# Expert selection beside the query products, and the gathered tile's second-table rows summed by TensorE

## The chip, the cores and the metric

One core of a Trainium2 chip runs the whole kernel. Its engines have queues of their own: TensorE (PE in the profile; its weight loads are PEld), VectorE (DVE), ScalarE (ACT), GpSimd (POOL) and SyncE (SP), which issues most transfers. The metric is the device time of one execution in microseconds, lower is better, compared by the median of several runs.

## The reference, cut to what matters

One layer over 512 tokens of width 2048: a token mixer (state space and pooling), and then an expert network, to which the change belongs. Each token has 8 heads; a head takes the best 16 of 128 first keys and of 128 second keys, sums them to 256 candidates and keeps the best 16, so a token has 128 picks among 128 x 128 single-neuron experts.

```python
q = (hb @ w_q).reshape(PEER_BLOCK, PEER_HEADS, 2, PEER_HALF)
s1 = jnp.einsum('thd,kd->thk', q[:, :, 0], k1).astype(jnp.float32)
s2 = jnp.einsum('thd,kd->thk', q[:, :, 1], k2).astype(jnp.float32)
v1, i1 = lax.top_k(s1, PEER_TOPK)
v2, i2 = lax.top_k(s2, PEER_TOPK)
...
top_s, pos = lax.top_k(cand, PEER_TOPK)
eid = jnp.take_along_axis(cid, pos, axis=-1)
g = jax.nn.softmax(top_s, axis=-1)
u_sel = jnp.take(u_tab, eid, axis=0)
act = jax.nn.gelu(jnp.einsum('td,thkd->thk', hb, u_sel).astype(jnp.float32)) * g
v_sel = jnp.take(v_tab, eid, axis=0)
return jnp.einsum('thk,thkd->td', act.astype(hb.dtype), v_sel)
```

The layer's output is x + g2 times this, followed by a final RMSNorm with weight final_w.

## The kernel before

The 512 tokens are four tiles of 128. All large products are done in three passes on operands split into a high and a low part (mm3, lines 109 to 112): `wload` (lines 117 to 132) loads a block of 128 x 1024 weights on SyncE's queue (wraw), ScalarE makes the high part (whi, line 125), and VectorE or GpSimd subtracts it to make the low part (wlo, line 126). Each wload is also a tick: side work is written as generators in lanes, and each tick advances a lane by its rate (line 199).

After the mixer come four stages. In `tail`, the output projection (accumulators pso), the second norm, and then the *query products* (psq, head by head) with their scores against the keys (pss). VectorE copies the scores out (sv) and GpSimd's queue sends them to a scratch in memory (scd).

`peer` is the expert network. Tiles 1 to 3 run dense: `dense_u` is the *expert scores* stage, products of the three tiles with the whole first table (psU, 384 columns, 128 second keys of two blocks each), and `dense_v` is the *weighted sum* stage, products with the whole second table (psV, 512 columns, 256 blocks). Tile 0 runs by gathered rows: `gather_tile` fetches for each pick one row of the first table for each of its 128 tokens (an indirect transfer of 1 MB issued by GpSimd), VectorE multiplies and sums it with the tokens (line 1095), ScalarE makes the weight, and then the row of the second table is fetched and VectorE adds it, weighted, to the tile's output (line 1088). This lane (lane0) runs through both stages at 0.29 and 0.25 picks a tick.

A second lane (lane1, 1.6 steps a tick) runs beside the expert scores: `topk` reads a tile's scores back and selects on VectorE (top16: five instructions for 8 + 8 values), tile 0 first; `dense_keys` and `dense_gates` then spread the dense tiles' gates with one-hot products (psd) into scratch. In both stages lo_pool gives the share of low parts that GpSimd makes, 0.5.

A scheduler orders each engine's instructions ahead of time by its own simulated timeline; on GpSimd, from `peer` on, the order is that of the code. At run time each engine works through its order. The gathered rows have three buffers (rows2), and psT are two PSUM banks for small results.

## Time and profile before

| | before |
|---|---|
| median of 3 runs | 3981.82 us |
| the runs | 3994.41, 3969.19, 3981.82 us |
| span of the profiled execution | 3959.9 us |
| busy: TensorE, VectorE, GpSimd, ScalarE | 3750.4, 2587.5, 1726.1, 1185.9 us |

The span runs from the first to the last instruction of the profiled execution. The execution's own device time is not listed on the page beside it; the runs without a profile lie 9.3 to 34.5 us above the span, the median 21.9 us. Times in the views are microseconds from the start of the span. The query products lie at 1391 to 1594 us, the expert scores from there to 2857, the weighted sum to 3942.

### The profile page before, as it was taken

Reading aid. Unit: us, or ns where it says so; the run is one execution under the profiler, and the core shown is the slowest. Engines: PE = TensorE matmul, PEld = TensorE weight load, DVE = VectorE, ACT = ScalarE, POOL = GpSimd, SP = SyncE. Lnnn points to the kernel's source line nnn. Section 1 sums busy time; section 2 is a strip of 40 time slices with the busy share of each in tenths; the row PEclk is TensorE's granted clock in tenths of the full one; section 3 lists DMA queues with packets and bytes.
Section 4 is the critical chain, followed back from the end, with each engine's and each line's share of the span. In section 5 each row is a group of like instructions: output and inputs, shape, how many; then the busy total and the mean of one; then the engine's idle time right before and its main releaser. Section 6 shows DMA issues by size and latency. Waiting matters only on the chain.

```text
span 3959.9 us, 49350 instructions
## 1 busy us (share of the span) xinstructions
PE 3750.4 (95%) x18841; PEld 3200.4 (81%) x18841; DVE 2587.5 (65%) x3347; ACT 1185.9 (30%) x1742; POOL 1726.1 (44%) x985
## 2 busy tenths in 40 slices
PE   5999998889899899999999999999999999999997
PEld 2478876667777778999999999999978788888886
DVE  5264379997563332899997777854666666566666
ACT  4123331112222222332333333323333333333332
POOL 0043125552322300355554344445566666666663
PEclk9999999989999999999999999999999999999999
DMA  8635658779865423477776777788888887888784
GB/s 270 212 120 185 206 169 232 222 221 302 241 223 186 141 86 112 149 255 272 281 263 254 272 262 275 256 297 297 302 306 293 311 296 284 306 312 292 281 310 173
DMA packets 458238, 962.81 MB, mean 243 GB/s; under 512 B 105040, under 2 KB 248784, under 8 KB 422416
## 3 DMA queue, kind: packets, MB, share of 16 engines
q1 hardware_dynamic: 380896, 588.77, 45.8%
q0 software_dynamic: 47744, 305.23, 20.7%
q10 hardware_dynamic: 29360, 65.64, 4.5%
q8 instruction: 148, 2.42, 0.3%
q14 instruction: 90, 0.74, 0.1%
HBM read 864.08 MB, written 99.12 MB: 243 GB/s over the span
## 4 chain that ended last, share of the span: by engine, by line
PE 54%; DVE 10%; DMA 3%; POOL 1%; issue 1%; SPq 0%; ACT 0%; DVEq 0%; POOLq 0%; ACTq 0%
PE psV L111 8%; PE psV L112 8%; PE psV L110 8%; PE psU L112 5%; PE psU L111 5%; PE psU L110 5%; PE psd L1151 3%; DVE wlo L126 2%; PE pso L111 2%; PE pso L110 2%; PE pso L112 2%; PE psq L111 1%; PE psq L112 1%; PE psq L110 1%; DMA row<-in_u,eid 1%; DVE row L1095 1%
## 5 line engine op out<-in xcount | busy, mean ns | idle before, releaser
L125 ACT CAST whi<-wraw 128x1024 fp32r<-128x1024 f32 x712 | 746.5, 1050 | 1779.0 <-PE psU L111 472.8
L126 DVE TENSOR_TENSOR wlo<-wraw,whi 128x1024 fp32r<-128x1024 f32 x456 | 643.8, 1412 | 648.4 <-ACT whi L125 307.6
L126 POOL TENSOR_TENSOR wlo<-wraw,whi 128x1024 fp32r<-128x1024 f32 x256 | 705.8, 2758 | 799.9 <-ACT whi L125 758.1
L112 PE MATMUL psU<-h2Th,wlo 128*128 128x384 f32 x2048 | 698.3, 341 | 28.6 <-DVE wlo L126 18.9
L110 PE MATMUL psU<-h2Th,whi 128*128 128x384 f32 x2048 | 698.8, 341 | 6.6 <-ACT whi L125 6.6
L111 PE MATMUL psU<-h2Tl,whi 128*128 128x384 f32 x2048 | 696.9, 340 | 0.0
L111 PE MATMUL psV<-wlo,ah 128*128 128x512 f32 x1536 | 606.5, 395 | 10.5 <-DVE wlo L126 5.9
L112 PE MATMUL psV<-whi,al 128*128 128x512 f32 x1536 | 605.4, 394 | 0.0
L110 PE MATMUL psV<-whi,ah 128*128 128x512 f32 x1536 | 554.4, 394 | 0.0
L112 PEld LDWEIGHTS psU<-h2Th,wlo 128*128 128x128 f32 x2048 | 389.7, 190 | 35.1 <-DVE wlo L126 23.2
L1095 DVE SCALAR_TENSOR_TENSOR row<-row,h 128x2048 f32<-128x2048 f32 x128 | 352.9, 2757 | 92.9 <-DMA row<-in_u,eid 92.9
L110 PEld LDWEIGHTS psU<-h2Th,whi 128*128 128x128 f32 x2048 | 391.1, 191 | 7.1 <-ACT whi L125 6.9
L111 PEld LDWEIGHTS psU<-h2Tl,whi 128*128 128x128 f32 x2048 | 390.2, 191 | 0.1
L111 PEld LDWEIGHTS psV<-wlo,ah 128*128 128x128 f32 x1536 | 289.8, 189 | 82.1 <-POOL wlo L126 8.3
L1088 DVE SCALAR_TENSOR_TENSOR ffn<-row,w,ffn 128x2048 f32<-128x2048 f32 x127 | 340.6, 2682 | 10.2 <-DMA row<-in_v,eid 10.2
L112 PEld LDWEIGHTS psV<-whi,al 128*128 128x128 f32 x1536 | 289.4, 188 | 67.0
L110 PEld LDWEIGHTS psV<-whi,ah 128*128 128x128 f32 x1536 | 289.1, 188 | 66.3
L1080 POOL DMA_INDIRECT row<-in_u,eid x128 | 209.0, 1633 | 247.7 <-ACT w L1096 97.5
L1080 POOL DMA_INDIRECT row<-in_v,eid x128 | 255.5, 1996 | 19.2 <-issue 7.0
L820 DVE SCALAR_TENSOR_TENSOR lacc<-lw,sil,lacc 128x512 f32<-128x512 f32 x240 | 213.6, 890 | 55.1 <-DMA lw<-in_w_mod 53.1
L112 PE MATMUL psg<-hhi,wlo 128*128 128x512 f32 x512 | 203.6, 402 | 25.5 <-DVE wlo L126 25.5
L110 PE MATMUL psg<-hhi,whi 128*128 128x512 f32 x512 | 203.8, 398 | 0.0
(350 smaller groups left out, 5537.2 us busy)
## 6 DMA issues: line engine op xcount, KB each, us to landing
wraw<-in_uT SPq DMA_DIRECT2D x256, 512.0 KB
wraw<-in_v SPq DMA_DIRECT2D x256, 512.0 KB
lw<-in_w_mod SPq DMA_DIRECT2D x256, 256.0 KB
wraw<-in_w_in SPq DMA_DIRECT2D x96, 512.0 KB
wmod<-in_w_mod SPq DMA_DIRECT2D x48, 512.0 KB
sd<-sev ACTq DMA_DIRECT2D x64, 384.0 KB
gds<-ast ACTq DMA_DIRECT2D x12, 2048.0 KB
sr<-sd SPq DMA_DIRECT2D x32, 768.0 KB
```

The source lines that it names most:

```text
L110: mm(ps, a.hi, b.hi, start=start, stop=False)
L111: mm(ps, a.hi, b.lo, start=False, stop=False)
L112: mm(ps, a.lo, b.hi, start=False, stop=stop)
L125: nc.scalar.copy(hi, raw)
L126: ins = (eng or nc.vector).tensor_tensor(lo, raw, hi.bitcast(F32), op=OP.subtract)
L820: nc.vector.scalar_tensor_tensor(acc, w, self.sil[:, k, 0:1], acc, op0=OP.mult, op1=OP.add)
L1080: nc.gpsimd.indirect_dma_start(out=r, out_offset=None, in_=I[tab], in_offset=bass.IndirectOffsetOnAxis(ap=eid[:, k:k + 1], axis=0))
L1088: V.scalar_tensor_tensor(acc, v, w, acc, op0=OP.mult, op1=OP.add)
L1095: V.scalar_tensor_tensor(u, u, 1.0, h2, op0=OP.mult, op1=OP.mult, accum_out=w[:, 0:1])
L1151: nc.tensor.matmul(ps[:, n * P:(n + 1) * P], oh[:, 0, :, n], R[:, q, :, n], start=(q == 0), stop=(q == 2))
```

## The change

The selection moves from `topk` into the loop over heads of the query products: ScalarE copies the scores, VectorE takes the best 16 of each of the four tiles' keys straight from the copy and then the best 16 of the candidates, head by head. The scratch scd, its writes and its reads are gone. The low parts of heads 1 to 7's query weights are made by GpSimd. What is left of `topk` (the keys of the picks and the softmax) is `picks`.

The gathered tile is worked in two halves. `gather_u`, beside the expert scores (lane0, 0.58 steps a tick), fetches all 128 rows of the first table and keeps the dot products; at the end it makes all weights at once and transposes weights and expert numbers, so that the picks lie on the partitions. `gather_v`, beside the weighted sum (0.56 steps a tick), fetches for each of the 128 *tokens* the 128 rows of the second table that it picked. A row block is then summed by TensorE: float32 products with a 128 x 32 weight tile (st) that is zero but for the column of this token, 512 columns each, one for each quarter of the 2048 output columns, at column positions 0, 32, 64 and 96 (psG). Groups of 32 tokens share an accumulator; at the end of each group the residual, the norm and the store follow in the same layout of quarters. In the weighted sum the share of GpSimd in the low parts falls from 0.5 to 0.34, and lane1 takes 1.1 steps a tick.

The core of the diff (comments that fell away are left out):

```diff
                 for kb in range(KT // 4):
-                    w = self.wchunk(I["peer_wq"], kb * 4, 4, hd * 256, 256)
+                    w = self.wchunk(I["peer_wq"], kb * 4, 4, hd * 256, 256, nc.gpsimd if hd else None)
                     for kk in range(4):
                         k = kb * 4 + kk
                         for j in range(2):
                             self.mm3(ps[j], w[:, kk, j * P:(j + 1) * P], h2T[:, k, :], k == 0, k == KT - 1)
                 for j in range(2):
-                    qt = ep.tile([P, SEQ], F32, tag="xr", name=self.nm("qt"), bufs=4)
+                    qt = ep.tile([P, SEQ], F32, tag="xr", name=self.nm("qt"))
                     nc.scalar.copy(qt, ps[j])
                     pss = self.psT.tile([P, 512], F32, tag="tr", name=self.nm("pss"))
                     for t in range(TT):
                         nc.tensor.matmul(pss[:, t * P:(t + 1) * P], qt[:, t * P:(t + 1) * P], self.kT[:, j, :], start=True, stop=True)
                     sv = ep.tile([P, SEQ], F32, tag="sv", name=self.nm("sv"))
-                    nc.vector.tensor_copy(sv, pss)
-                    nc.gpsimd.dma_start(self.scd[:, :, (hd * 2 + j) * P:(hd * 2 + j + 1) * P].rearrange("t p k -> p t k"),
-                                        sv.rearrange("p (t k) -> p t k", t=TT))
+                    nc.scalar.copy(sv, pss)
+                    for t in range(TT):
+                        junk = ep.tile([P, 256], F32, tag="tkj", name=self.nm("tkj"))
+                        self.top16(self.vv[t][:, hd, j], self.ii[t][:, hd, j], sv[:, t * P:(t + 1) * P], junk[:, 0:P])
+                for t in range(TT):
+                    cand = ep.tile([P, TOPK, TOPK], F32, tag="cand", name=self.nm("cand"))
+                    shp = [P, TOPK, TOPK]
+                    nc.vector.tensor_tensor(cand, self.vv[t][:, hd, 0].unsqueeze(2).broadcast_to(shp),
+                                            self.vv[t][:, hd, 1].unsqueeze(1).broadcast_to(shp), op=OP.add)
+                    junk = ep.tile([P, 256], F32, tag="tkj", name=self.nm("tkj"))
+                    self.top16(self.ts[t][:, hd], self.pos[t][:, hd], cand.rearrange("p a b -> p (a b)"), junk)
...
-        S = tp.tile([P, 2 * HEADS, P], F32, tag="S", name=self.nm("S"))
-        nc.sync.dma_start(S, self.scd[t].rearrange("p (h k) -> p h k", k=P))
...
-    def gather_tile(self, t, res, acc):
-        nc, I, V, h2 = self.nc, self.I, self.nc.vector, self.h2[t]
+    def gather_u(self, t, res, out):
+
+
+        nc, I, V, kp, h2 = self.nc, self.I, self.nc.vector, self.keep, self.h2[t]
         i1, i2, g = res[t]
-        ef = self.keep.tile([P, NK], F32, name=self.nm("ef"))
+        ef = kp.tile([P, NK], F32, name=self.nm("ef"))
         V.scalar_tensor_tensor(ef, i1, float(P), i2, op0=OP.mult, op1=OP.add)
-        eid = self.keep.tile([P, NK], I32, name=self.nm("eid"))
+        eid = kp.tile([P, NK], I32, name=self.nm("eid"))
         V.tensor_copy(eid, ef)
-
-        def row(tab, k):
-            r = self.rowp.tile([P, D], F32, tag="row", name=self.nm("row"))
-            nc.gpsimd.indirect_dma_start(out=r, out_offset=None, in_=I[tab],
-                                         in_offset=bass.IndirectOffsetOnAxis(ap=eid[:, k:k + 1], axis=0))
-            return r
-
-        def vacc(k, v, w):
-            if k == 0:
-                V.tensor_scalar(acc, v, w, None, op0=OP.mult)
-            else:
-                V.scalar_tensor_tensor(acc, v, w, acc, op0=OP.mult, op1=OP.add)
-
-        u, pend = row("u", 0), None
+        dots = kp.tile([P, NK], F32, name=self.nm("dots"))
+        u = self.row("u", eid, 0)
         yield
         for k in range(NK):
+            nxt = self.row("u", eid, k + 1) if k + 1 < NK else None
             with self.tc.issue_after(self.last_lo):
-                w = self.sm.tile([P, 4], F32, tag="w", name=self.nm("w"))
-                V.scalar_tensor_tensor(u, u, 1.0, h2, op0=OP.mult, op1=OP.mult, accum_out=w[:, 0:1])
-                nc.scalar.activation(w[:, 1:2], w[:, 0:1], AF.Gelu_apprx_tanh)
-                nc.scalar.activation(w[:, 2:3], w[:, 1:2], AF.Copy, scale=g[:, k:k + 1])
-                if pend is not None:
-                    vacc(*pend)
-            v = row("v", k)
-            pend = (k, v, w[:, 2:3])
-            if k + 1 < NK:
-                u = row("u", k + 1)
+                V.scalar_tensor_tensor(u, u, 1.0, h2, op0=OP.mult, op1=OP.mult, accum_out=dots[:, k:k + 1])
+            u = nxt
             yield
-        vacc(*pend)
...
+        nc.scalar.activation(dots, dots, AF.Gelu_apprx_tanh)
+        V.tensor_tensor(dots, dots, g, op=OP.mult)
+        ps = self.psT.tile([P, 512], F32, tag="tr", name=self.nm("pst"))
+        for j, x in enumerate((dots, ef)):
+            nc.tensor.transpose(ps[:, j * P:(j + 1) * P], x, self.ident)
+        wT = kp.tile([P, P], F32, name=self.nm("wT"))
+        nc.scalar.copy(wT, ps[:, 0:P])
+        eT = kp.tile([P, P], I32, name=self.nm("eT"))
+        V.tensor_copy(eT, ps[:, P:2 * P])
+        out.append((wT, eT))
+        yield
+
+    def row(self, tab, ids, k):
+        r = self.rowp.tile([P, D], F32, tag="row", name=self.nm("row"))
+        self.nc.gpsimd.indirect_dma_start(out=r, out_offset=None, in_=self.I[tab],
+                                          in_offset=bass.IndirectOffsetOnAxis(ap=ids[:, k:k + 1], axis=0))
+        return r
+
...
+        wT, eT = wt[0]
+        st = [kp.tile([P, 32, 32], F32, name=self.nm("st")) for _ in range(2)]
+        for x in st:
+            nc.vector.memset(x, 0.0)
...
+        rows = [self.row("v", eT, k) for k in range(2)]
+        yield
+        for g in range(4):
+            s = st[g % 2]
+            V.tensor_copy(s.rearrange("p a b -> p (a b)")[:, 0:32 * 32:33], wT[:, g * 32:(g + 1) * 32])
+            ps = self.psT.tile([P, 512], F32, tag="tr", name=self.nm("psG"))
+            for j in range(32):
+                k = g * 32 + j
+                if k + 2 < P:
+                    rows.append(self.row("v", eT, k + 2))
+                r = rows.pop(0)
+                for q in range(4):
+                    nc.tensor.matmul(ps[32 * q:32 * q + 32, :], s[:, j, :], r[:, q * 512:(q + 1) * 512],
+                                     start=(j == 0), stop=(j == 31), tile_position=(0, 32 * q))
+                yield
+            r0 = t * P + g * 32
+            x1 = kp.tile([P, 512], F32, tag="x1q", name=self.nm("x1q"))
+            for q in range(4):
+                nc.sync.dma_start(x1[32 * q:32 * q + 32], self.x1d[r0:r0 + 32, q * 512:(q + 1) * 512])
+            o = kp.tile([P, 512], F32, tag="outq", name=self.nm("outq"))
+            V.tensor_tensor(o, ps, g2, op=OP.mult)
+            V.tensor_tensor(o, o, x1, op=OP.add)
+            ss = self.sm.tile([P, 4], F32, tag="ssq", name=self.nm("ssq"))
+            nc.scalar.activation(x1, o, AF.Square, accum_out=ss[:, 0:1])
+            ps = self.psT.tile([P, 512], F32, tag="tr", name=self.nm("psn"))
+            nc.tensor.matmul(ps[:, 0:1], same.rearrange("p q j -> p (q j)"), ss[:, 0:1], start=True, stop=True)
+            nc.scalar.activation(ss[:, 1:2], ps[:, 0:1], AF.Sqrt, bias=self.epsb, scale=1.0 / D)
+            V.reciprocal(ss[:, 2:3], ss[:, 1:2])
+            V.scalar_tensor_tensor(o, o, ss[:, 2:3], fw, op0=OP.mult, op1=OP.mult)
+            for q in range(4):
+                nc.sync.dma_start(self.out[r0:r0 + 32, q * 512:(q + 1) * 512], o[32 * q:32 * q + 32])
             yield
-            self.add_half(t, acc, dh, self.ss[0])
-        yield
-        self.finish(t, acc, self.ss[0])
 
...
-                yield from self.topk(tp, 0, res)
-                self.lane0[2].append(self.gather_tile(0, res, acc0))
+                yield from self.picks(self.tkp, 0, res)
+                self.lane0[2].append(self.gather_u(0, res, wt))
                 for t in DT:
-                    yield from self.topk(tp, t, res)
+                    yield from self.picks(self.tkp, t, res)
                     yield from self.dense_keys(t, res, ix)
...
-            self.lane0 = lane0 = self.lane(0.29, [])
-            lane1 = self.lane(1.6, [prep()])
+            self.lane0 = lane0 = self.lane(0.58, [])
+            lane1 = self.lane(1.1, [prep()])
...
-            lane0[0], self.lo_pool = 0.25, 0.5
+            lane0, self.lo_pool = self.lane(0.56, [self.gather_v(0, wt)]), 0.34
```

How the change stands in the engines' orders, at three places. First TensorE early in the weighted sum, at the change from one weight block to the next (psV are the accumulators, ah and al the split weights of the experts, whi and wlo the table's block). Before:

```order
L111 MATMUL psV_23277<-wlo_23451,ah_23278 128x512
L112 MATMUL psV_23277<-whi_23450,al_23279 128x512
L110 MATMUL psV_23272<-whi_23474,ah_23278 128x512
L110 MATMUL psV_23273<-whi_23474,ah_23278 128x512
L110 MATMUL psV_23274<-whi_23474,ah_23278 128x512
```

And now, at the same products:

```order
L111 MATMUL psV_23099<-wlo_23301,ah_23100 128x512
L112 MATMUL psV_23099<-whi_23300,al_23101 128x512
L1138 MATMUL psG_23211<-row_23212,st_23139 32x512 x4
L110 MATMUL psV_23094<-whi_23324,ah_23100 128x512
L110 MATMUL psV_23095<-whi_23324,ah_23100 128x512
L110 MATMUL psV_23096<-whi_23324,ah_23100 128x512
```

The four quarter products of one token's rows stand between two blocks; the weighted sum's own products are as many as before.

Second, VectorE at the start of the expert scores. Before, the scores of the last head are copied out, the low part of the third second key's first block follows (wlo_12122), and tile 0's selection comes behind it:

```order
L126 TENSOR_TENSOR wlo_11956<-wraw_11954,whi_11955 128x1024
L126 TENSOR_TENSOR wlo_12041<-wraw_12039,whi_12040 128x1024
L1006 COPY sv_11895<-pss_11890 128x512
L1006 COPY sv_11905<-pss_11900 128x512
L126 TENSOR_TENSOR wlo_12122<-wraw_12120,whi_12121 128x1024
L1019 MAX vv_11962<-S_11960 128x8 x6
L1020 MAX_INDEX ii_11963<-vv_11962,S_11960 128x8
```

Now (ts and pos are the best candidates of a tile, oh and rf belong to picks, wlo_12669 is the low part of the fourth block that TensorE takes):

```order
L1033 MAX_INDEX pos_10799<-ts_10795,cand_12552 128x8
L1034 MATCH_REPLACE tkj_12554<-ts_10795,cand_12552 128x256
L1048 CAST rf_12604<-ri_12601 128x256
L1035 MAX ts_10794<-tkj_12546 128x8
L1035 MAX ts_10795<-tkj_12554 128x8
L1052 TENSOR_TENSOR oh_12607<-rf_12604,iota 128x2048
L1036 MAX_INDEX pos_10798<-ts_10794,tkj_12546 128x8
L1036 MAX_INDEX pos_10799<-ts_10795,tkj_12554 128x8
L1055 TENSOR_TENSOR oh_12607<-oh_12607,iif_12599 128x2048
L126 TENSOR_TENSOR wlo_12669<-wraw_12667,whi_12668 128x1024
```

The low part now stands behind the last head's selection of all four tiles and behind two steps of picks for tile 0.

Third, GpSimd in the weighted sum. Before (rows of both tables in turn, between low parts):

```order
L1080 DMA row_24599<-in_v,eid_12933 128x2048
L1080 DMA row_24601<-in_u,eid_12933 128x2048
L126 TENSOR_TENSOR wlo_24663<-wraw_24661,whi_24662 128x1024
L126 TENSOR_TENSOR wlo_24711<-wraw_24709,whi_24710 128x1024
L1080 DMA row_24720<-in_v,eid_12933 128x2048
L1080 DMA row_24722<-in_u,eid_12933 128x2048
```

And now (sr is the product of scores and gates of the dense tiles):

```order
L1245 TENSOR_TENSOR sr_23938<-sr_23938,gr_23939 128x12x4x32
L126 TENSOR_TENSOR wlo_24074<-wraw_24072,whi_24073 128x1024
L1102 DMA row_24078<-in_v,eT_22265 128x2048
L1102 DMA row_24108<-in_v,eT_22265 128x2048
L126 TENSOR_TENSOR wlo_24158<-wraw_24156,whi_24157 128x1024
```

Rows of the second table alone are fetched, by the transposed expert numbers (eT), and one low part stands between two pairs of rows where there were two.

## Rows read from the trace of the kernel before

**Rows 1.** The page, busy time, share of the span and instructions of each engine.

```profile
PE 3750.4 (95%) x18841; PEld 3200.4 (81%) x18841; DVE 2587.5 (65%) x3347; ACT 1185.9 (30%) x1742; POOL 1726.1 (44%) x985
```

**Rows 2.** The windows view, by stage (start:end, length, then by column).

```profile
core 0: us, PE busy (x) PEld busy (x) DVE busy (x) ACT busy (x) POOL busy (x), PEclk, DMA share, GB/s
1391.50:1594.00 202.50, 201.02 (x965) 167.22 (x964) 63.45 (x68) 47.92 (x60) 13.22 (x16) 1.00 0.32 100
1594.00:1970.00 376.00, 354.34 (x1963) 349.36 (x1962) 347.99 (x797) 118.43 (x167) 180.32 (x77) 0.97 0.69 243
1970.00:2620.00 650.00, 641.52 (x4026) 626.74 (x4025) 510.45 (x602) 221.12 (x350) 289.14 (x131) 0.99 0.73 264
2620.00:2857.00 237.00, 228.22 (x1298) 226.75 (x1297) 119.33 (x73) 74.72 (x112) 125.65 (x58) 0.99 0.84 301
2857.00:3942.00 1085.00, 1072.74 (x4611) 867.32 (x4609) 693.92 (x453) 342.60 (x420) 687.76 (x282) 1.00 0.80 290
3942.00:3960.00 18.00, 0.00 (x0) 0.00 (x0) 13.34 (x18) 4.22 (x9) 0.00 (x0) 0.52 0.52 204
```

**Rows 3.** The windows view of one tile each: psV, psU (PE, PEld, others), psd.

```profile
3100.00:3300.00 200.00, 199.95 (x863) 161.86 (x863) 11.44 (x18) 1.00 0.85 310
...
2700.00:2780.00 80.00, 78.49 (x452) 78.17 (x451) 4.34 (x9) 1.00 0.81 293
...
2420.00:2600.00 180.00, 42.82 (x324) 15.64 (x27) 1.00 0.75 268
```

**Rows 4.** The waits view of TensorE, 1594 to 2857: total us, times, longest.

```profile
PE psU L112 <- DVE wlo L126: 18.9, 9, 4.0
PE psU L112 <- POOL wlo L126: 9.6, 7, 3.0
```

**Rows 5.** The same, 2857 to 3960.

```profile
PE psV L111 <- DVE wlo L126: 5.9, 2, 4.9
PE psV L111 <- POOL wlo L126: 4.6, 6, 1.7
```

**Rows 6.** The groups by line, VectorE, 2857 to 3960: busy, mean ns, idle before.

```profile
L1095 DVE SCALAR_TENSOR_TENSOR row<-row,h 128x2048 f32<-128x2048 f32 x61 | 190.4, 3122 | 50.8 <-DMA row<-in_u,eid 50.7
...
L1088 DVE SCALAR_TENSOR_TENSOR ffn<-row,w,ffn 128x2048 f32<-128x2048 f32 x62 | 175.3, 2828 | 9.5 <-DMA row<-in_v,eid 9.5
```

**Rows 7.** The windows view of tile vv (first level), then of ts (second).

```profile
1594.00:2120.00 526.00, 103.88 (x516) 0.97 0.70 247
...
1594.00:2120.00 526.00, 68.69 (x260) 0.97 0.70 247
```

**Rows 8.** The groups by line, 1391 to 1594, VectorE's own.

```profile
L126 DVE TENSOR_TENSOR wlo<-wraw,whi 128x1024 fp32r<-128x1024 f32 x32 | 40.7, 1273 | 104.3 <-PE psq L112 99.2 <-ACT whi L125 5.1
...
L1006 DVE COPY sv<-pss 128x512 f32<-128x512 f32 x16 | 11.1, 691 | 30.1 <-PE pss L1004 30.1
```

**Rows 9.** The timeline of TensorE, first stage: start us, us, instruction.

```profile
107.97 0.39 PE L110 MATMUL psz<-whi,chi 128*128 128x512 f32 x1
108.28 1.05 PE L244 MATMUL psmod<-wmod,silz 128*32 128x512 f32 x4
...
109.61 0.40 PE L112 MATMUL psz<-whi,clow 128*128 128x512 f32 x1
```

**Rows 10.** The same, earlier (L343 is a float32 transpose).

```profile
42.21 0.62 PE L244 MATMUL psmod<-wmod,silz 128*32 128x256 f32 x4
42.77 1.09 PE L343 MATMUL pst<-ident,xt 128*128 128x128 f32 x8
...
45.37 1.06 PE L244 MATMUL psmod<-wmod,silz 128*32 128x256 f32 x12
```

**Rows 11.** The transfers, 2857 to 3942: issues, median us to landing.

```profile
row<-in_v,eid POOLq DMA_INDIRECT x61, 8.9
```

**Rows 12.** The timeline of TensorE in the query products (39 starts apart).

```profile
1455.09 0.39 PE L110 MATMUL psq<-h2Th,whi 128*128 128x512 f32 x1
...
1464.02 0.39 PE L110 MATMUL psq<-h2Th,whi 128*128 128x512 f32 x1
```

More of the change, by code (lines that the diff above doesn't have):

```diff
@@ L284, in mixers @@
         self.x1d = self.dram.tile([SEQ, D], F32, name="x1d")
-        self.scd = self.dram.tile([TT, P, 2 * HEADS * P], F32, name="scd")
         es_h, es_b = self.es(), self.es()
@@ L990, in tail @@
             self.h2T = h2T = Split(th, tl)
+            es_x.close()
+            ep = es.enter_context(pool(name="ev4", bufs=2))
+            self.es_e, self.es_t = self.es(), self.es()
+            self.evp = self.es_e.enter_context(pool(name="sev", bufs=2, side="right"))
+            self.tkp = tkp = self.es_t.enter_context(pool(name="topk", bufs=1, side="right"))
+            self.vv = [tkp.tile([P, HEADS, 2, TOPK], F32, name=f"vv{t}") for t in range(TT)]
+            self.ii = [tkp.tile([P, HEADS, 2, TOPK], U32, name=f"ii{t}") for t in range(TT)]
+            self.ts = [tkp.tile([P, HEADS, TOPK], F32, name=f"ts{t}") for t in range(TT)]
+            self.pos = [tkp.tile([P, HEADS, TOPK], U32, name=f"pos{t}") for t in range(TT)]
             for hd in range(HEADS):
@@ new lines, in tail, with top16, picks @@
+        self.check("q")
+    def top16(self, vals, idx, src, junk):
+        V = self.nc.vector
+        V.max(out=vals[:, 0:8], in_=src)
+        V.max_index(out=idx[:, 0:8], in_max=vals[:, 0:8], in_values=src)
+        V.match_replace(out=junk, in_to_replace=vals[:, 0:8], in_values=src, imm_value=-3.0e38)
+        V.max(out=vals[:, 8:16], in_=junk)
+        V.max_index(out=idx[:, 8:16], in_max=vals[:, 8:16], in_values=junk)
+    def picks(self, tp, t, res):
+        nc, V = self.nc, self.nc.vector
+        ts, pos, shp = self.ts[t], self.pos[t], [P, HEADS, TOPK, TOPK]
+        iif = tp.tile([P, HEADS, 2, TOPK], F32, tag="iif", name=self.nm("iif"))
+        V.tensor_copy(iif, self.ii[t])
@@ new lines, in quarters, with gather_v @@
+    def quarters(self, pool, ap, name):
+        t = pool.tile([P, 512], F32, name=name)
+        for q in range(4):
+            self.nc.sync.dma_start(t[32 * q:32 * q + 32], ap[:, q * 512:(q + 1) * 512].broadcast_to([32, 512]))
+        return t
+    def gather_v(self, t, wt):
+        nc, I, V, kp = self.nc, self.I, self.nc.vector, self.keep
+        wT, eT = wt[0]
+        st = [kp.tile([P, 32, 32], F32, name=self.nm("st")) for _ in range(2)]
+        for x in st:
+            nc.vector.memset(x, 0.0)
+        g2, fw = self.quarters(kp, self.modd[:, 3 * D:4 * D], "g2q"), self.quarters(kp, I["final_w"], "fwq")
+        same = kp.tile([P, 4, 32], F32, name="same")
+        V.tensor_reduce(same[:, 0], self.ident.rearrange("p (q j) -> p j q", q=4), axis=AX.X, op=OP.add)
+        for q in range(1, 4):
+            V.tensor_copy(same[:, q], same[:, 0])
+        rows = [self.row("v", eT, k) for k in range(2)]
[27 more added lines that the diff above has]
+            V.scalar_tensor_tensor(o, o, ss[:, 2:3], fw, op0=OP.mult, op1=OP.mult)
+            for q in range(4):
+                nc.sync.dma_start(self.out[r0:r0 + 32, q * 512:(q + 1) * 512], o[32 * q:32 * q + 32])
@@ L1325, in peer @@
             es_k.close()
-        self.hp.close()
 def build(tc, I, out, dbg=None, stop=None):
```

48 lines of the change are left out of this document (11 added, 37 removed).

## The prediction, made before the changed kernel ran

> **What bounds the kernel now.** I read the first part of the page first: TensorE is busy for 95% of the span and VectorE for 65% [rows 1]; the median of the runs, 3981.8 us, lies 21.9 us above that span. A share of busy time says little by itself, so I cut the span into stages with the windows view [rows 2]. The reader is to see that TensorE is busy for 201.0 of the 202.5 us of the query products, for 1224.1 of the 1263 us of the expert scores (three windows), and for 1072.7 of the 1085 us of the weighted sum; the granted clock is 0.97 to 1.00 there, which is the 2.4 GHz level. VectorE is over 90% busy only in the first window of the scores (348.0 of 376 us).
>
> Busy TensorE need not be TensorE at its pace, so I priced one product in the windows where nothing is late [rows 3]: 200.0/863 = 0.232 us for one of the weighted sum (512 columns), 78.5/452 = 0.174 us for one of the scores (384 columns), 42.8/324 = 0.132 us for a spread-gate product. The weighted sum has 3 x 1536 = 4608 products: 4608 x 0.232 = 1069 of its 1085 us. The scores' windows hold 7287 products; 1152 of them are the spread gates' (3 tiles, 128 tokens, 3 parts), so 6135 x 0.174 + 1152 x 0.132 = 1067 + 152 = 1219 of 1263 us. So, whatever is taken off the other engines, TensorE can get back about 44 us in the scores and 16 us in the weighted sum. The waits agree: 28.5 us of idle TensorE in the scores were ended by a low part of a weight block, and 10.5 us in the weighted sum [rows 4, 5]. TensorE is the bound from the queries on, and the tail of 18 us behind it stays as it is.
>
> **What is taken away.** VectorE loses the products with the second table's rows: 175.3 us in the weighted sum, and a like time in the scores; the dot products with the first table's rows (190.4 us in the weighted sum) all move into the scores, where they take the place of the row sums that leave [rows 6]. In the weighted sum VectorE, now 693.9 us busy, falls to 693.9 - 175.3 - 190.4 = 328 us, plus some 40 low parts that the new share (0.34 on GpSimd instead of 0.5) hands back to it. None of this was on the path: of the 12.3 us that TensorE idles there, 10.5 us are late low parts. I credit 6 us; the bounds are 0 and 12.
>
> **The selection.** It moves beside the query products. Today its two levels take 103.9 + 68.7 = 172.6 us of VectorE (the sums of candidates are among them) [rows 7]. The query stage gives VectorE 202.5 us and uses 63.5; the change takes away 28 of 32 low parts at 1.273 us and 16 copies of 11.1 us in all [rows 8], so VectorE would hold 63.5 - 35.6 - 11.1 + 172.6 = 189 us there. Per head that is 21.6 us of selection beside 25.3 us of products: it keeps up, and TensorE waits for none of it, since the low parts of heads 1 to 7 are on GpSimd and ScalarE copies the scores. I cost the stage at nothing; the cover is thin, and if it is gone, each microsecond that a head's selection takes over 25.3 us holds back the second of the two score buffers, then ScalarE's next high part, then TensorE.
>
> The end of the stage is where it shows. The last head's selection, 21.6 us, starts when its scores exist, that is when TensorE is already in the expert scores. In the order of VectorE's instructions the fourth block of the scores (its low part is wlo_12669 in the order above) stands behind nearly all of it and two steps of the picks. TensorE reaches that block after 72 products, 72 x 0.174 = 12.5 us; VectorE after about 21.6 + 5 + 1.3 = 28 us: a wait of some 16 us. The next blocks stand behind steps of the picks, for some 15 us more. Against this goes what the selection costs today in the same place: the first window of the scores has 376 us for 1963 products of 0.174 us = 341 us, 35 us lost. So nearly a wash: I credit 5 us, with bounds of 40 us gained (the selection out of the way, the boundary hidden) and 15 us lost.
>
> **The new products.** This is the term that decides. For each of the 128 tokens of the gathered tile TensorE now does four float32 products, 32 weight columns by 512 columns, one for each quarter of the output's columns, at four column positions. The trace of before has this form in the first stage: 32-column float32 products of the conditioning. Two of them, 512 columns, are four records (two passes each) over 1.05 us, and they stand between products that otherwise start every 0.23 us: from the product at 107.97 to that at 109.61 us are 1.64 us, where two starts would take 0.46, so the pair costs 1.18 us of TensorE's time [rows 9]. Do products at different positions run side by side? A full-width float32 transpose is two passes of 128 columns; four of them take 1.09 us, so a pass takes about 0.11 us, 0.22 for 256 columns. A pair at 256 columns, four passes, took 0.62 us, where one after the other would be 0.9: two run at once, a round of 0.43 and a fixed 0.19. Do four? Six such products at alternating positions (0 and 32, then 64 and 96) took 1.06 us, which is two rounds and 0.19, where pairs alone would need three (1.48) [rows 10]. So four at different positions run as one round, and a token costs 1.18 us. In TensorE's new order 118 tokens stand as one group of four; ten are broken by other products into 24 pieces, so 142 groups: 142 x 1.18 = 168 us. The bounds are the bare rounds of 512 columns, 128 x 0.86 = 110 us, and pairs that don't overlap with other pairs, 128 x 2 x 1.18 = 302 us; I take the row's price, being that of the same form. Nothing hides them: they are on the engine that sets the end, in a stage with 16 us to spare. The change breaks even only at (44 + 16)/128 = 0.47 us a token.
>
> The Trainium skill, page "TensorE: Matmul & The Clock Gate", section "Part 3: Packing small matmuls", speaks against the full packing: it gives a measured speedup of 2.38 for three column tiles of 32 with 512 columns, so a pack takes 3/2.38 = 1.26 times one product. By that, as an estimate, a group would take 1.05 x 1.26 + 0.13 = 1.45 us and the term 206 us instead of 168. The row with six products shows no such surcharge, and no run here shows four at 512 columns.
>
> Around them: four small products for the norms and two transposes, under 2 us. The gathers themselves do not grow: 128 rows a stage where there were about 130, and a row lands 8.9 us after its issue [rows 11]. TensorE now waits for rows itself, and 18 products of the weighted sum queue behind each late one. In the new order a row's products stand at least 54 products, 12.5 us, behind the group that frees its buffer, mostly 90 to 108 (over 20 us); so few are late. On GpSimd a row's issue waits for that group too, and behind it wait the low parts; they are needed 55 products (12.7 us) later or more, in which an issue and a low part fit. I cost this at nothing, with an upper bound in the rivals.
>
> **The sum.** 168 + 2 - 6 - 5 = +159 us: a span of about 4119 us, and with the 21.9 us that lie around it 4141 us, 4.0% slower. The low end takes the pieces as free (128 x 1.05 = 134), the full 40 us in the scores and 12 in the weighted sum: +82. For the high end I let a quarter of the 118 whole groups run as pairs, since the rows leave the four-wide round at 512 columns open: (142 + 30) x 1.18 = 203, + 2 + 15 = +220.
>
> **The rivals.** (a) *TensorE's pace rises.* At one column a cycle of the 2.4 GHz level 512 columns would be 0.213 us, and the weighted sum's product takes 0.232: 4608 x 0.019 = 86 us that could be operands arriving late while VectorE and GpSimd, both some 64% busy there, use the same memory. With VectorE at half its load they could come back; with these and both stages' bounds (12 and 40 us instead of 6 and 5) the sum is 159 - 86 - 41 = +32 us, 4014 us: not slower. It decides from the point where most of those 0.019 us go. Against it: the query products have 512 columns too, with VectorE 31% and GpSimd 7% busy, and their pace is 8.93/39 = 0.229 us [rows 12], so hardly 0.003 us a product, 14 us, hang on the neighbours' load. (b) *The four don't pack.* Pairs only: 302 - 9 = +293, 4275 us; no packing, with some 1 us for each, +450. For it: the row of six is one place, at 256 columns; against it: that row has no room for three rounds. (c) *TensorE waits for rows.* If every third token waited 3 us for its rows or for a low part behind an issue, 128 us come on top: 4270 us. For it: transfers already take 80% of the stage's DMA time; against it: the slack in the order. (d) *Selection bounds the queries.* If a head's selection took 30 us instead of 21.6, 8 x 4.7 = 38 us: 4180 us, inside the range.
>
> **How the numbers follow.** This kernel's runs spread over 0.6%, so a change within 1% can hardly be told from none; I count 3942 to 4022 us as no change. Forecast with its own sizes, (d) among them: 0.80. (a): 0.10, of which 0.07 within 1% and 0.03 faster (more of the pace than its bound). (b): 0.05. (c): 0.05. Slower by over 1% is then 0.90. The range, 4055 to 4215 us, is the forecast's low and high end, 4064 and 4202, with some 10 us for the spread of the runs; it leaves out (a), (b) and (c).
>
> **What would show it.** The weighted sum lasts about 1245 us instead of 1085, with TensorE still over 98% busy; the groups of four take 1.05 us each and cost 1.18 between neighbours; 2.3 would mean pairs. VectorE falls below 450 us there. The query stage stays at 200 to 206 us with VectorE about 190 us busy; the first 100 us of the scores show TensorE waiting some 30 us for low parts behind the selection. What would make it wrong: a group that costs well under 1 us, or TensorE's idle time in the weighted sum rising by tens of microseconds on rows of the second table.

## The result and the profile after

The changed kernel takes 4111.07 us (median of 4 runs, 4104.01 to 4114.26), the kernel before 3978.79 us beside it: ratio 1.0337, 95% interval 1.0316 to 1.0358. It is slower by 132 us; 4141 us were forecast, range 4055 to 4215. The profiled execution of the changed kernel took 4114.26 us with a span of 4112.5 us.

The first part of the page after, beside [rows 1]: TensorE is busy for 163 us more, VectorE for 384 us less.

```profile
PE 3913.5 (95%) x19875; PEld 3211.8 (78%) x19875; DVE 2203.2 (54%) x3264; ACT 1136.1 (28%) x1505; POOL 1571.2 (38%) x956
```

The windows view after, by the same stages as [rows 2]: query products, three windows of the scores, weighted sum, tail.

```profile
core 0: us, PE busy (x) PEld busy (x) DVE busy (x) ACT busy (x) POOL busy (x), PEclk, DMA share, GB/s
1402.20:1600.60 198.40, 196.37 (x929) 162.31 (x928) 152.78 (x711) 54.23 (x72) 67.44 (x28) 0.99 0.24 81
1600.60:1980.00 379.40, 353.81 (x2090) 346.25 (x2090) 310.08 (x393) 113.65 (x149) 179.33 (x77) 0.97 0.71 248
1980.00:2620.00 640.00, 639.34 (x3940) 626.30 (x3940) 429.20 (x425) 201.73 (x265) 292.70 (x139) 1.00 0.76 274
2620.00:2854.30 234.30, 228.81 (x1296) 227.81 (x1296) 77.12 (x63) 67.64 (x83) 89.26 (x42) 0.99 0.68 240
2854.30:4092.90 1238.60, 1235.65 (x5642) 881.28 (x5641) 382.05 (x317) 317.49 (x305) 510.57 (x248) 1.00 0.75 258
4092.90:4112.50 19.60, 0.00 (x0) 0.00 (x0) 15.09 (x20) 4.22 (x9) 0.00 (x0) 0.62 0.48 187
```

The reader is to see where the time went: the weighted sum has 1238.6 us instead of 1085 (+153.6), and TensorE is busy for all but 3 us of them. The scores have 1253.7 instead of 1263 (-9.3), the query products 198.4 instead of 202.5 (-4.1), the tail 1.6 more. That makes +142; the query products also begin 10.7 us later (1402.2, not 1391.5). They began between 1395.9 and 1405.0 us in all nine experiments, and at 1398.8 in the second, which edits nothing ahead of the scores, so I take most of these 10.7 us for the spread of that long first part. The difference of the medians, 132 us, is smaller than the 152.6 between the two spans, because the profiled execution of before lay under the median of its kernel.

The timeline of TensorE after, in the weighted sum: one group of four products among the large ones, and then a piece of a group that large products cut, a single product of two records.

```profile
3302.95 0.40 PE L111 MATMUL psV<-wlo,ah 128*128 128x512 f32 x1
3303.18 0.40 PE L112 MATMUL psV<-whi,al 128*128 128x512 f32 x1
3303.51 1.07 PE L1138 MATMUL psG<-row,st 128*32 128x512 f32 x8
3304.50 0.50 PE L110 MATMUL psV<-whi,ah 128*128 128x512 f32 x1
3304.84 0.40 PE L111 MATMUL psV<-wlo,ah 128*128 128x512 f32 x1
```

```profile
3171.70 0.40 PE L110 MATMUL psV<-whi,ah 128*128 128x512 f32 x1
3172.03 1.04 PE L1138 MATMUL psG<-row,st 128*32 128x512 f32 x2
3173.00 0.50 PE L111 MATMUL psV<-wlo,ah 128*128 128x512 f32 x1
3173.34 0.40 PE L112 MATMUL psV<-whi,al 128*128 128x512 f32 x1
```

From the start at 3303.18 to that at 3304.84 are 1.66 us, where two starts take 0.46: the group costs 1.20 us, beside 1.18 from the pair in [rows 9]. Four products (8 records) take what two took there. The single product costs nearly as much: from 3171.70 to 3173.34 are 1.64 us, 1.18 beyond two starts. Counted like this over the whole stage, 103 groups that stand alone cost 1.20 us each and 15 pieces that stand alone 1.18 to 1.19, whether they hold one, two or three products; in 12 places a group stands directly behind another group or a piece, and the two together cost 2.04 to 2.06. Between groups the large products keep their pace of [rows 3]; 33 starts lie between these two rows of the same view, 7.63/33 = 0.231 us:

```profile
3230.76 0.40 PE L111 MATMUL psV<-wlo,ah 128*128 128x512 f32 x1
...
3238.39 0.39 PE L111 MATMUL psV<-wlo,ah 128*128 128x512 f32 x1
```

The waits view of TensorE after, scores and then weighted sum (total us, times, longest), beside [rows 4, 5]:

```profile
PE psU L112 <- DVE wlo L126: 27.6, 9, 12.4
PE psU L110 <- ACT whi L125: 3.1, 3, 1.5
PE psU L112 <- POOL wlo L126: 0.9, 1, 0.9
```

```profile
PE psV L111 <- DVE wlo L126: 2.0, 1, 2.0
PE psV L110 <- ACT whi L125: 0.6, 1, 0.6
PE psV L111 <- POOL wlo L126: 0.3, 1, 0.3
```

No row of the second table is waited for. The idle time of the weighted sum has almost gone, and it was small beside what was put on TensorE.

### The profile page after: what moved, and what is told of

Same layout as the page of the kernel before. It is cut to its first block, busy times and chain, and to the rows that moved or that the text cites. A ratio compares the mean times of both kernels' runs of the same rounds, so it can differ in the third digit from the quotient of the medians.

```text
span 4112.5 us, 50903 instructions
## 1 busy us (share of the span) xinstructions
PE 3913.5 (95%) x19875; PEld 3211.8 (78%) x19875; DVE 2203.2 (54%) x3264; ACT 1136.1 (28%) x1505; POOL 1571.2 (38%) x956
## 4 chain that ended last, share of the span: by engine, by line
PE 60%; DVE 3%; DMA 1%; issue 0%; POOL 0%; ACT 0%; DVEq 0%; ACTq 0%
PE psV L110 9%; PE psV L112 9%; PE psV L111 9%; PE psU L112 8%; PE psU L111 8%; PE psU L110 8%; PE psG L1138 3%; PE psd L1198 3%; PE psq L112 1%; PE psq L110 1%; PE psq L111 1%; DMA row<-in_u,eid 1%; DVE row L1085 1%; DVE wlo L126 1%; DVE oh L1055 0%
## 5 line engine op out<-in xcount | busy, mean ns | idle before, releaser
L126 POOL TENSOR_TENSOR wlo<-wraw,whi 128x1024 fp32r<-128x1024 f32 x243 | 628.5, 2587 | 1255.6 <-ACT whi L125 1072.0
L110 PE MATMUL psV<-whi,ah 128*128 128x512 f32 x1536 | 605.8, 403 | 0.6 <-ACT whi L125 0.6
L1085 DVE SCALAR_TENSOR_TENSOR row<-row,h 128x2048 f32<-128x2048 f32 x128 | 338.9, 2648 | 202.4 <-DMA row<-in_u,eid 202.2
L1102 POOL DMA_INDIRECT row<-in_v,eT x128 | 187.3, 1463 | 252.4 <-PE psG L1138 228.6
L111 PE MATMUL psg<-hlow,whi 128*128 128x512 f32 x512 | 203.3, 397 | 0.0
```

What stands on the lines that cost most here:

```text
L110: mm(ps, a.hi, b.hi, start=start, stop=False)
L111: mm(ps, a.hi, b.lo, start=False, stop=False)
L126: ins = (eng or nc.vector).tensor_tensor(lo, raw, hi.bitcast(F32), op=OP.subtract)
L1085: V.scalar_tensor_tensor(u, u, 1.0, h2, op0=OP.mult, op1=OP.mult, accum_out=dots[:, k:k + 1])
L1102: self.nc.gpsimd.indirect_dma_start(out=r, out_offset=None, in_=self.I[tab], in_offset=bass.IndirectOffsetOnAxis(ap=ids[:, k:k + 1], axis=0))
```

## The experiments

The stages in this table run from the first product of one to the first of the next (the weighted sum to the last product's start), taken from the windows view of each profile; cut like this, the stages of before have 196.7, 1268.9 and 1082.7 us.

| kernel | median us | ratio to before (95%) | queries | scores | weighted sum |
|---|---|---|---|---|---|
| changed kernel | 4111.1 | 1.0337 (1.0316 to 1.0358) | 193.3 | 1258.8 | 1238.2 |
| 1 selection alone | 3965.3 | 0.9977 (0.9960 to 0.9993) | 193.9 | 1260.2 | 1089.7 |
| 2 TensorE sums alone | 4129.1 | 1.0392 (1.0354 to 1.0430) | 196.9 | 1267.1 | 1238.3 |
| 3 sums on VectorE | 3954.6 | 0.9946 (0.9928 to 0.9964) | 192.9 | 1247.0 | 1086.4 |
| 4 groups kept together | 4095.4 | 1.0301 (1.0264 to 1.0338) | 193.4 | 1257.8 | 1226.1 |
| 5 products twice | 4209.5 | 1.0585 (1.0513 to 1.0656) | 193.7 | 1261.9 | 1337.0 |
| 6 one column position | 4420.3 | 1.1115 (1.1053 to 1.1177) | 192.9 | 1260.8 | 1544.6 |
| 7 two quarters | 4093.1 | 1.0292 (1.0240 to 1.0344) | 194.2 | 1256.6 | 1222.8 |
| 8 low parts on VectorE | 4107.2 | 1.0327 (1.0277 to 1.0378) | 197.8 | 1252.1 | 1238.2 |
| 9 sums on VectorE, share 0.5 | 3962.3 | 0.9968 (0.9951 to 0.9985) | 193.3 | 1253.2 | 1093.9 |

My theory: TensorE sets the end, four products run as one round, and the round plus a fixed price for leaving and re-entering the large products is the whole loss. The rivals: the products run in pairs, the loss is a wait, or it comes from the selection.

**1. The selection alone**, with the gathered tile of before, and **2. the sums alone**, with the selection of before.

```diff
 # 1: from the changed kernel
-                self.lane0[2].append(self.gather_u(0, res, wt))
+                self.lane0[2].append(self.gather_tile(0, res, acc0))
...
 # 2: from the kernel before
-                self.lane0[2].append(self.gather_tile(0, res, acc0))
+                self.lane0[2].append(self.gather_u(0, res, wt))
...
```

The code of the two forms of the gathered tile and their rates are left out here; they are those of the change.

> The selection beside the query products alone, with the old gathered tile (row sums of both tables on VectorE, no products of TensorE for them). Theory (the selection costs TensorE nothing and relieves the expert scores; the whole slowdown is the new products): the query stage stays at 198 to 206 us, the expert scores lose 5 to 25 us, the weighted sum stays at 1083 to 1087 us; the median is 0.1% to 0.6% under the kernel before. Rival (the selection bounds the query products, or only pushes its work into the scores): the query stage takes 230 us or more, or the time is above the kernel before by over 0.5%.

> The old selection from the scratch, with the gathered tile in two halves and the second table's rows summed by TensorE. Theory (the new products are a bare addition to TensorE's time): the weighted sum takes 1230 to 1245 us instead of 1085, the scores stay within 20 us of 1263; 145 to 165 us above the kernel before, ratio 1.036 to 1.042. Rival (part of the loss comes from the selection's new place): under 110 us above.

The selection alone gains 12 us by the medians; its interval excludes 1. In its profile the scores are 8.7 us shorter, as expected, but the weighted sum is 7.0 us longer than before (1089.7 us, above the expected 1083 to 1087), 4.3 us of it a wait for a VectorE sum out of the accumulators. The sums alone came out as expected: they cost 152 us, and their weighted sum is the changed kernel's to 0.1 us. Together that makes 140 us, beside 132 measured (the ends of its interval are 0.0316 and 0.0358 of 3978.8 us, 126 and 142). So within the spread the two halves add up, they have opposite signs, and the loss is all in the sums.

**3. The second table's rows summed by VectorE again**, with everything else of the change kept.

```diff
-                for q in range(4):
-                    nc.tensor.matmul(ps[32 * q:32 * q + 32, :], s[:, j, :], r[:, q * 512:(q + 1) * 512],
-                                     start=(j == 0), stop=(j == 31), tile_position=(0, 32 * q))
+                    V.scalar_tensor_tensor(acc, r, w[:, k:k + 1], acc, op0=OP.mult, op1=OP.add)
...
```

> The changed kernel with one thing undone: in the weighted sum the second table's rows are fetched by picks and summed by VectorE, with the weights made ahead; selection, two halves and rates stay. Theory (what the change loses are TensorE's products alone): the weighted sum goes back to 1073 to 1088 us although VectorE then carries some 650 us instead of 490, and the time is 15 to 30 us below the kernel before: faster than both. Rival (the slowdown comes from the order of the halves, the row transfers or the shares of the low parts): the weighted sum stays over 1120 us.

As the theory had it: 22.8 us faster than before, and by the medians faster than every other kernel here. Its windows, scores and weighted sum:

```profile
1591.40:2838.40 1247.00, 1218.09 (x7343) 1196.70 (x7342) 814.34 (x889) 384.30 (x496) 556.59 (x257) 0.99 0.74 261
2838.40:3924.80 1086.40, 1056.85 (x4610) 864.78 (x4608) 731.47 (x434) 317.03 (x298) 576.23 (x248) 1.00 0.83 294
```

VectorE carries 731 us in the weighted sum, 350 more than in the changed kernel, and the stage is 152 us shorter. The gain over before lies in the scores (-22 us): TensorE idles 28.9 us there (1247.0 - 1218.1), beside 38.9 before; the other 12 us are in its busy time.

The length of the weighted sum hides two things that oppose each other. TensorE idles 29.6 us of it (1086.40 - 1056.85), where it idled 10.5 before and 3.0 in the changed kernel. And its large products follow each other faster; there are 33 starts between these two rows of its timeline, 7.48/33 = 0.227 us:

```profile
3230.58 0.39 PE L111 MATMUL psV<-wlo,ah 128*128 128x512 f32 x1
...
3238.06 0.39 PE L111 MATMUL psV<-wlo,ah 128*128 128x512 f32 x1
```

Over 4608 products the difference to the changed kernel's 0.231 is some 20 us. In the scores the pace is quicker too (0.1733 us from start to start instead of 0.1741, some 5 us of the 12). The ninth experiment has the same 0.227 us; the first, which also sums these rows on VectorE, keeps 0.232. So VectorE's load does not make the difference, and no run here shows what does. The 152 us are therefore not the bare price of the new products: the longer waits (27 us) and the quicker pace cancel in large part, which is luck. The order of the halves and the transfers of rows, here by picks, are cleared of the loss by this run.

**4. The four products kept together** by the scheduler, and **5. each set issued twice** (weights halved).

```diff
 # 4
+                with self.tc.high_priority(offset=400):
                 for q in range(4):
 # 5
+                for h in range(2):
                 for q in range(4):
-                                     start=(j == 0), stop=(j == 31), tile_position=(0, 32 * q))
+                                     start=(j == 0 and h == 0), stop=(j == 31 and h == 1), tile_position=(0, 32 * q))
...
```

> The changed kernel with the four products of a token kept together by the scheduler: no token's group is split by other products, 128 groups instead of 142. Theory (a change from the large products to a group costs a fixed part beside the products themselves): 14 groups fewer at 0.13 us of fixed cost, and each round of 1.05 us spent once instead of twice, so 10 to 17 us below the changed kernel. Rival (pieces cost only their own share): within 3 us of it.

> The changed kernel with each token's four products issued twice, one set behind the other, with halved weights. Theory (the products are on the path and a group's time is the products' own): 127 further groups at 0.9 to 1.07 us, since the fixed part at the change from and to the large products is paid once: 114 to 136 us above the changed kernel, the weighted sum at 1350 to 1375 us. Rival 1 (the loss is a wait at the change or a wait for rows): under 40 us above. Rival 2 (the products run in pairs): 250 us or more above.

Kept together, the weighted sum is 12.1 us shorter, by the medians 15.7, as expected: 14 rounds fewer at 0.87 us, the price found below, are 12.2 us. The doubled set came out under its expectation, +98.8 us in the weighted sum where at least 114 was expected. The timeline of TensorE with the doubled sets says why:

```profile
3301.91 1.92 PE L1139 MATMUL psG<-row,st 128*32 128x512 f32 x16
```

One set takes 1.06 us and two take 1.92, so the second adds 0.86. And in the order of this kernel the products of 127 of the 128 tokens stand together, as in the fourth experiment and not as in the changed kernel; the fourth is its proper partner. Against it the second sets cost 1337.0 - 1226.1 = 110.9 us, 0.87 us each. So a token's price is 0.87 us for the round, and for the passage from the large products and back what is left: the fourth experiment's stage is 1226.1 us, of which 4608 x 0.2317 = 1067.7 are large products and 2.9 idle time (1226.1 - 1223.2), so 155.5/128 = 1.21 us a token, the norms in it, and 1.21 - 0.87 = 0.34 us for the passage. The expectation had spread the passage too thin (0.13 us) and so made the round too dear.

**6. All four products at the first column position**, and **7. only two of the four products.** Each keeps the full four at the first token of 32; the first adds the four quarters up in one place, the second leaves out half of the columns.

```diff
 # 6
+                    c = q if j == 0 else 0
-                    nc.tensor.matmul(ps[32 * q:32 * q + 32, :], s[:, j, :], r[:, q * 512:(q + 1) * 512],
+                    nc.tensor.matmul(ps[32 * c:32 * c + 32, :], s[:, j, :], r[:, q * 512:(q + 1) * 512],
 # 7
-                for q in range(4):
+                for q in (range(4) if j == 0 else range(2)):
...
```

> The changed kernel, in which the four products of a token (but the first of each 32) all go to the first column position, so that none can run beside another; the four quarters are added up there, so the output is another one. Theory (the four run as one round at four positions, and one round of 512 columns takes some 0.9 us): a token costs 3.4 to 3.8 us instead of 1.2, so 124 x 2.2 to 2.6 = 270 to 325 us above the changed kernel. Rival (the four never packed, a float32 product is simply 0.26 us): within 15 us of it.

> The changed kernel with only two of the four products of a token (all four for the first of each 32); the second half of the output's columns is left out of the sum. Theory (four run as one round, so the time is that of one): the weighted sum stays within 12 us of the changed kernel's. Rival (they run as two rounds of pairs): 124 x 0.45 to 0.55 = 55 to 70 us below it.

The timeline of TensorE, one token in the sixth and one in the seventh:

```profile
3306.82 3.62 PE L1139 MATMUL psG<-row,st 128*32 128x512 f32 x8
```

```profile
3307.68 1.05 PE L1138 MATMUL psG<-row,st 128*32 128x512 f32 x4
```

At one position the same eight records take 3.62 us instead of 1.07: the stage grows by 306 us. (3.62 - 1.07)/3 = 0.85 us is what a product costs that can't run beside another. And two products at two positions take 1.05 us, what four take; the stage is 15 us below the changed kernel's, three more than was allowed, but only 3.3 us below that of the fourth experiment, whose groups are whole. In the seventh almost all are, and they make 116 stretches between large products instead of 128; 12 passages at 0.34 us are 4 us. This settles the disputed step: four at four positions are one round at 512 columns, and the rival of pairs is dead. The pieces of one product in the changed kernel, 1.18 us beside 1.20 for four, say the same.

**8. The low parts of all heads' query weights on VectorE**, 28 of them beside the selection.

```diff
-                    w = self.wchunk(I["peer_wq"], kb * 4, 4, hd * 256, 256, nc.gpsimd if hd else None)
+                    w = self.wchunk(I["peer_wq"], kb * 4, 4, hd * 256, 256)
```

> The changed kernel with the low parts of all heads' query weights on VectorE again, 28 of them beside the selection. Theory (the cover over the selection is thin: a head has 25 us of products, the selection takes some 20 us of VectorE, four low parts of 1.27 us come on top and stand behind selection steps): the query stage grows by 10 to 30 us. Rival (the selection has slack enough): within 4 us of the changed kernel's 198 us.

My theory of a thin cover fell. The query stage grows by 4.5 us, half a microsecond over the rival's bound and far under 10; the scores shrink by 6.7, the time stays. The windows of the query stage, changed kernel and then this one:

```profile
1402.20:1595.50 193.30, 191.27 (x907) 158.03 (x906) 147.68 (x692) 53.41 (x71) 67.44 (x28) 0.99 0.25 82
```

```profile
1396.40:1594.20 197.80, 196.33 (x927) 162.34 (x925) 170.41 (x734) 54.13 (x72) 0.00 (x0) 0.99 0.26 83
```

VectorE gets 28 low parts of 1.22 us (34 us), yet its busy time rises by 23 only. The sums of candidates explain the difference: together they take 24.4 us in the changed kernel and 13.3 here. Their group, changed kernel and then this one (ns min/median/max):

```profile
L1022 DVE TENSOR_TENSOR cand<-vv x32: 395/406/2141, 1453.1 to 1620.2; 128x256 f32<-128x256 f32 x32
```

```profile
L1022 DVE TENSOR_TENSOR cand<-vv x32: 403/417/433, 1450.2 to 1614.0; 128x256 f32<-128x256 f32 x32
```

With GpSimd idle none of them takes over 0.44 us; in the changed kernel 11 of the 32 take 0.98 to 2.14.

**9. The third kernel with GpSimd's share of the low parts at 0.5.**

```diff
-            lane0, self.lo_pool = self.lane(0.56, [self.gather_v(0, wt)]), 0.34
+            lane0, self.lo_pool = self.lane(0.56, [self.gather_v(0, wt)]), 0.5
```

> The kernel of the third experiment (second table's rows summed by VectorE, weights ahead) with GpSimd's share of the low parts in the weighted sum back at 0.5 from 0.34. There TensorE idled about 30 us in the weighted sum, 17.7 us of it for low parts and 10.4 us for a VectorE copy out of the accumulators. Theory (VectorE, 731 us busy, is late because of the low parts it was given for a lighter load; some 40 of them go back to GpSimd): these waits halve, the weighted sum takes 1072 to 1080 us, the time is 5 to 14 us below the third experiment's 3954.6. Rival (the waits come from ScalarE's high parts and the transfers, not from VectorE's load): within 4 us of it.

This theory fell too: the weighted sum is 7.5 us longer, not shorter, and the rival's 4 us are passed as well. The groups by line of VectorE in the weighted sum, third kernel and then this one (busy us, mean ns):

```profile
L1119 DVE SCALAR_TENSOR_TENSOR ffn<-row,dots,ffn 128x2048 f32<-128x2048 f32 x127 | 336.3, 2648 | 19.8 <-DMA row<-in_v,eid 19.5
L126 DVE TENSOR_TENSOR wlo<-wraw,whi 128x1024 fp32r<-128x1024 f32 x167 | 265.8, 1596 | 286.3 <-ACT whi L125 285.9
```

```profile
L1119 DVE SCALAR_TENSOR_TENSOR ffn<-row,dots,ffn 128x2048 f32<-128x2048 f32 x127 | 356.7, 2808 | 47.7 <-DMA row<-in_v,eid 47.3
L126 DVE TENSOR_TENSOR wlo<-wraw,whi 128x1024 fp32r<-128x1024 f32 x127 | 202.0, 1591 | 276.9 <-ACT whi L125 276.6
```

VectorE gives up 40 low parts (64 us), and its busy time falls by 14 only (717 us beside 731), since its other operations grow longer. TensorE's waits in the weighted sum, third kernel and then this one (total us, times, longest):

```profile
PE psV L111 <- DVE wlo L126: 12.4, 9, 2.4
PE psV L110 <- DVE ffn L1247: 10.4, 6, 2.6
PE psV L111 <- POOL wlo L126: 5.0, 7, 1.4
PE psV L110 <- ACT whi L125: 1.5, 3, 0.6
```

```profile
PE psV L110 <- DVE ffn L1247: 12.5, 6, 3.4
PE psV L111 <- POOL wlo L126: 11.3, 9, 3.2
PE psV L110 <- ACT whi L125: 8.3, 4, 3.4
PE psV L111 <- DVE wlo L126: 0.8, 2, 0.4
```

The waits only change their cause: from low parts of VectorE to those of GpSimd and to ScalarE's high parts. By the medians the share of 0.34 is the better of the two, by 8 us; the intervals of their ratios overlap a little.

## Why the prediction was right, step by step

**The bound and the new products.** Both right. TensorE had no room in the weighted sum, and the term of 142 groups x 1.18 = 168 us is 1238.6 - 1067.7 - 3.0 idle = 168 us, the norms in it. Its parts are a little off and cancel: a whole group costs 1.20 us, and 12 of the 142 stand behind another without a passage of their own, so that the groups alone come to 165.7 us. (The whole stage grew by 153.6: against the 168 stand 9.3 us less idle time and 5 us that TensorE spent on the old products beyond 1067.7.) That the row of the pair gave the right price was partly luck in its parts: the bare round was rightly read from the transposes (0.86; 0.87 and 0.85 measured), but the fixed part, 0.19 us in my reading of the records, is 0.34 us between large products. The measured pair of [rows 9] held both. Four-wide packing at 512 columns, which the prediction left open, is shown by the sixth and seventh experiments. The estimate from the Trainium skill, page "TensorE: Matmul & The Clock Gate", section "Part 3: Packing small matmuls", 1.45 us a group and 206 us, is not borne out: the trace has 1.20 us a group between its neighbours and 168 us. What failed is the step from a speedup to a longer pack. Here four products take 3.62 us at one position and 1.07 at four, a speedup of 3.4, and yet they are one round: some 0.2 us of fixed part stand in both times.

**What is taken from VectorE.** The forecast was 6 us of waits, and 9.3 came back (12.3 us of idle time before, 3.0 after). VectorE falls to 382 us, as expected below 450.

**The selection.** The direction was right, and its size too small: the term of 5 us is 13 us between the profiles (queries -4.1, scores -9.3) and 12 by the medians of the first experiment, though in that experiment's profile the weighted sum gives 7.0 us back. VectorE has 148 to 153 us of work in the query stage, not 189: 172.6 us were put there whole, but about 28 us of them (12.5 on tile vv and 15.3 on ts) fall into the scores with the last head, and all of it takes 166 us (101.4 and 64.7 on the two tiles). That the cover was thin was wrong, by the eighth experiment. The wait at the boundary came as described, and smaller: in the first 104.5 us of the scores 20.0 us are waits (17.5 of them for VectorE's low parts, the longest 12.4), about 30 were forecast. The longest has a tail that the prediction did not count: behind it the granted clock stands at 0.50, the 1.2 GHz level, and 12 products take 0.33 us each instead of 0.174 (window, its length, busy time of TensorE, clock, and two columns on transfers):

```profile
1627.50:1635.50 8.00, 3.97 (x12) 0.50 0.48 143
```

That is some 2 us.

**The sum.** By stages 142 us (+153.6 - 9.3 - 4.1 + 1.6) where 159 were forecast; the median says 132. The low end leaves out the 2 us for the norms (+84, not +82). Between the two profiles the spans differ by 152.6 us, 10.7 of them ahead of the query products. What was off in the forecast time of 4141 us is the base above all: I put 21.9 us around the span. The execution behind the span of 4112.5 us took 4114.26, so 1.8 us lie around it, and if the same holds for before, its profiled execution was some 17 us below the median of its kernel. In which stage those 17 us lie in the other executions no profile shows.

**The rivals.** (a) No pace came back in the changed kernel: 0.231 us a product with VectorE at half its load. A quarter of the 0.019 us came back in the third and ninth kernels, where VectorE is as busy as before, so not by this rival's mechanism. (b) Dead, above; with all four at one position the time is 446 us above before, beside the +450 that was put for no packing. (c) No wait for rows; a row's issue on GpSimd waited for TensorE 63 times, 228.6 us, and TensorE waited 0.3 us for GpSimd in the weighted sum. (d) Dead by the eighth experiment.

## What to carry to other kernels

An engine with spare time is not a reason to relieve it: work moved to the engine that sets the end is paid in full, here 1.2 us a token, beside 2.65 us of VectorE that cost TensorE some 0.2 us in waits (27 us for 128 tokens, third experiment). Price a small product on a full TensorE between its neighbours, start to start, and not by its own record, since the passage from the large products and back costs two fifths of a round more. When a change has two halves, run each alone: here the selection was worth keeping and was hidden under a loss twelve times its size.

## What was not expected of the hardware

I had not expected a short sum of two operands on VectorE to stand still while GpSimd makes a low part. The timeline of the changed kernel shows one case:

```profile
1452.57 2.41 POOL L126 TENSOR_TENSOR wlo<-wraw,whi 128x1024 fp32r<-128x1024 f32 x1 [3.09 <-PE psq L112]
1453.12 2.14 DVE L1022 TENSOR_TENSOR cand<-vv 128x256 f32<-128x256 f32 x1
```

The sum of candidates starts 0.55 us after the low part and ends 0.28 us after its end (1454.98, 1455.26), 2.14 us instead of 0.41. The eighth experiment, with no low part on GpSimd there, has a longest one of 0.433 us, so the neighbour causes it. All 32 sums agree: the 11 long ones each start inside a low part of GpSimd and end 0.28 to 0.29 us after it, and none of the other 21 overlaps one. The other instructions of the selection keep their 0.28 or 0.41 us; 179 of them start inside a low part, and the longest took 0.437. It also fits that in the ninth experiment a row sum takes 2.81 us instead of 2.65 when GpSimd has 41 low parts more. For such pairs, work handed to GpSimd comes back to VectorE in part, as longer operations. The Trainium skill, page "SBUF — State Buffer", section "Who interferes with whom", has this rule: a VectorE instruction that reads two operands from that memory shares an interface with GpSimd's reads, and the one that comes second waits until the first is through. The trace agrees (2.14 us beside a low part, 0.433 at most without one). The rule's other half is that an instruction with at most one such operand is left alone, outside the modes that use both of VectorE's ports; the trace agrees here too (the 179 above).
